# A mixture-of-experts decoder layer on one core: slot weights in the experts' middle layer, the last pair's rows by a one-hot product, the branch at the end, shorter planned waits

## The chip, the cores and the metric

One core of a Trainium2 chip. The time is the device time of one execution in microseconds (us); where several runs are shown, their median. The engines are TensorE (PE, with its weight loads as PEld), VectorE (DVE), ScalarE (ACT), GpSimd (POOL) and SyncE (SP), which here issues the DMA transfers. Each engine works through its own list of instructions in order, and semaphores tie the lists together.

## The reference, cut to what matters

One layer of a decoder over 512 tokens of 1024 channels. An input projection feeds three token mixers (RWKV-7, block-sparse attention, an S5 state space), their outputs are gated, summed and projected; a layer norm follows. Then a router picks one of four groups and in it two of eight experts for each token:

```
def rwkv7_mixer(...): y = wkv7_scan(r, decay, k, v, -kk, kk * a); group norm over heads; (y + bonus) * g
merged = gates0 * (y_a @ w_up_rwkv) + gates1 * (y_b @ w_up_moba) + gates2 * (y_c @ w_up_ssm)
x = layer_norm(alpha * x + merged @ w_out)
weight = p_group * softmax(top2(e_logits))                # two per token
hid = silu(xb @ w_gate[e]) * (xb @ w_up[e])               # expert: 1024 -> 256
y[token] += (hid @ w_down[e]) * weight                    # both experts of a token
x = layer_norm(alpha * x + y)
```

The weight is a number per token and expert, so it may be multiplied into the hidden row as well as into the output row. All is float32; large products are split in a high and a low part of a shorter format and done as three products.

## The kernel before, in words

**The mixers.** The projections with the three mixers take the first 612 us. TensorE's list is written out in a fixed order by a small planner (`Trunk.run`): several generators, such as `rwkv`, `rwkv_ends` and `rwkv_next`, put out their work and yield a planned wait in us. The planner's clock is `PE.t`, which each matmul advances by columns x passes / 2400. When no generator is due, it takes the next piece of *fill*: gate and up-projection matmuls that nothing waits for, three per 128x128 block of split weights (`xhi,whi`, `xlo,whi`, `xhi,wlo`; later with `y`, then `b`, operands). When the fill is used up, the clock is set ahead and TensorE waits. The fill's weights are split into `whi` on ScalarE and `wlo` on GpSimd (line 304 and 305), a few ahead.

RWKV runs in two halves of four heads. In each, `rwkv_inv` inverts 32x32 blocks on DVE (31 steps of a product, L601, and a sum, L602, then transposes into TT and DF, L605 and L607), yields `46.0`, and has TensorE use DF; `rwkv_chain` carries the state S through eight chunks and writes Ys; `rwkv_post` normalises Ys by group, yields 21.0, transposes it on TensorE and adds into yfA (L717 to L719, over a buffer `yt`). `merge_parts` reads the results yd of the other two mixers back through a buffer `yf`, eight times, and splits each into hi (ACT) and lo (POOL: ylo, blo).

```
for s in range(31):  ... v.tensor_tensor(tm, LA[...], TL[...], op=mult); v.tensor_tensor(TL[...], TL[...], tm, op=add)
v.transpose(DF[:32], TT[:32, :, :32])
yield 46.0
```

**The experts.** After the output projection, norm and routing (612 to 696 us), 32 experts run as 16 pairs; each expert has 64 places, and a pair fills the 128 partitions. `slots()` makes tables by one-hot matmuls: for each place the slot row (`dst`, two rows per token) and the token (`src`). GpSimd gathers a pair's tokens two pairs ahead (`fetch`), TensorE turns them (`turn`), `hidden` runs the first matmuls and the middle layer, `outputs` the second, and an indirect DMA scatters the 128 rows to `ybuf` in DRAM. Weights (`expert_weights`: up 2 x 2 MB, down 2 x 1 MB per pair) stream through slots on SP's queue, in 1 MB transfers. An expert with more than 64 tokens is finished in `more_blocks`, behind a branch on a number `nov` read from SBUF; with these inputs it is 0. `combine` then reads the two rows of each token back, adds them to x1 by matmuls with two diagonal matrices of the weights (`dg`), and normalises.

## Time and profile before

| | |
|---|---|
| median of 3 runs | 978.24 us (973.08 to 980.92) |
| the profiled execution | 970.03 us, span 968.3 us |
| mean granted TensorE clock | 0.971 of full speed |
| TensorE busy | 862.3 us (89%) |
| DVE, ACT, POOL busy | 547.6, 320.6, 306.4 us |
| expert weights | 96 transfers of 1 MB |

Times in the rows are from the start of the span. A timeline row has start, duration, engine, line, operation and names, and in brackets the engine's idle time before it with what ended it. The time is about 2 us longer than the span, which is what lies around it.

### The profile page before, as it was taken

Reading aid. Unit: us, or ns where it says so; the run is one execution under the profiler, and the core shown is the slowest. Engines: PE = TensorE matmul, PEld = TensorE weight load, DVE = VectorE, ACT = ScalarE, POOL = GpSimd, SP = SyncE. Lnnn points to the kernel's source line nnn. Section 1 sums busy time; section 2 is a strip of 40 time slices with the busy share of each in tenths; the row PEclk is TensorE's granted clock in tenths of the full one; section 3 lists DMA queues with packets and bytes.
Section 4 is the critical chain, followed back from the end, with each engine's and each line's share of the span. In section 5 each row is a group of like instructions: output and inputs, shape, how many; then the busy total and the mean of one; then the engine's idle time right before and its main releaser. Section 6 shows DMA issues by size and latency. Waiting matters only on the chain. (4 is left out here: it accounts for less than half of the span.)

```text
span 968.3 us, 13711 instructions
## 1 busy us (share of the span) xinstructions
PE 862.3 (89%) x4988; PEld 577.7 (60%) x4988; DVE 547.6 (57%) x1348; ACT 320.6 (33%) x626; POOL 306.4 (32%) x265
## 2 busy tenths in 40 slices
PE   6998897899999999799999968988979997879775
PEld 4876665677877776678788756866643333323232
DVE  6999998345325899625996776548631110101117
ACT  4244545576337157321532202232001110101012
POOL 6462512232453333622355213553001111101003
PEclk9999999999999999999999988999999999989998
DMA  6821322141442212321256312589798999999955
GB/s 209 166 97 55 66 86 57 50 141 59 138 131 66 87 66 71 125 78 56 89 154 207 120 65 66 175 340 386 290 367 346 413 417 420 419 419 418 409 200 187
DMA packets 71016, 186.62 MB, mean 193 GB/s; under 512 B 22027, under 2 KB 22027, under 8 KB 58624
## 3 DMA queue, kind: packets, MB, share of 16 engines
q1 hardware_dynamic: 66048, 175.77, 50.5%
q0 software_dynamic: 4896, 9.93, 2.7%
q8 instruction: 41, 0.67, 0.3%
q14 instruction: 31, 0.25, 0.1%
HBM read 171.29 MB, written 22.28 MB: 200 GB/s over the span
## 5 line engine op out<-in xcount | busy, mean ns | idle before, releaser
L305 POOL TENSOR_TENSOR wlo<-raw,whi 128x512 fp32r<-128x512 f32 x156 | 214.8, 1382 | 345.1 <-ACT whi L304 334.2
L175 PE MATMUL bank<-xhi,whi 128*128 128x512 f32 x400 | 168.9, 422 | 8.6 <-ACT whi L304 7.5
L175 PE MATMUL bank<-xhi,wlo 128*128 128x512 f32 x400 | 159.9, 400 | 7.6 <-POOL wlo L305 7.3
L304 ACT ACTIVATE whi<-raw 128x512 fp32r<-128x512 f32 x156 | 97.5, 628 | 200.4 <-PE bank L175 136.1
L175 PE MATMUL bank<-xlo,whi 128*128 128x512 f32 x400 | 159.7, 399 | 2.0 <-DVE xlo L305 1.9
L175 PE MATMUL bank<-we,xgT 128*64 128x512 f32 x512 | 127.5, 624 | 17.5 <-DMA we<-in_ex 17.5
L175 PEld LDWEIGHTS bank<-we,xgT 128*64 128x64 f32 x512 | 42.0, 144 | 98.7 <-issue 72.2
L175 PEld LDWEIGHTS bank<-xhi,whi 128*128 128x128 f32 x400 | 77.5, 194 | 28.9 <-ACT whi L304 7.9
L175 PEld LDWEIGHTS bank<-xhi,wlo 128*128 128x128 f32 x400 | 76.8, 192 | 27.8 <-POOL wlo L305 11.4
L175 PEld LDWEIGHTS bank<-xlo,whi 128*128 128x128 f32 x400 | 77.0, 193 | 17.9 <-DVE xlo L305 4.4
L1618 DVE SCALAR_TENSOR_TENSOR eth<-eth,bank 128x256 f32<-128x256 f32 x16 | 6.7, 421 | 129.1 <-ACT eth L1617 129.0
L175 PE MATMUL bank<-we,hT 128*64 128x512 f32 x256 | 59.2, 598 | 8.4 <-ACT hT L1629 7.3
L1617 ACT ACTIVATE eth<-bank 128x256 f32<-128x256 f32 x16 | 6.1, 384 | 162.4 <-PE bank L175 162.4
L1593 POOL DMA_INDIRECT xg<-x1d,src x14 | 14.2, 1018 | 121.3 <-PE bank L179 98.9
L1642 POOL DMA_INDIRECT ybuf<-we,dst x16 | 16.2, 1009 | 94.5 <-issue 42.1
L175 PEld LDWEIGHTS bank<-we,hT 128*64 128x64 f32 x256 | 18.9, 136 | 38.4 <-issue 25.0
L1641 DVE COPY we<-bank 128x512 f32<-128x512 f32 x16 | 11.1, 691 | 54.1 <-PE bank L175 54.1
L175 PE MATMUL bank<-wlo,mxhi 128*128 128x512 f32 x64 | 25.6, 400 | 3.2 <-POOL wlo L305 3.2
L784 ACT ACTIVATE s<-s,st 128x128 f32<-128x128 f32 (+3 forms) x32 | 17.8, 557 | 31.2 <-DVE st L783 31.2
L175 PE MATMUL bank<-whi,mxhi 128*128 128x512 f32 x64 | 25.9, 405 | 0.9 <-ACT whi L304 0.9
L175 PE MATMUL bank<-yhi,whi 128*128 128x512 f32 x64 | 25.8, 404 | 0.3 <-ACT yhi L304 0.3
L175 PE MATMUL bank<-ylo,whi 128*128 128x512 f32 x64 | 25.3, 395 | 0.8 <-POOL ylo L305 0.8
(466 smaller groups left out, 1596.8 us busy)
## 6 DMA issues: line engine op xcount, KB each, us to landing
we<-in_ex SPq DMA_DIRECT2D x96, 1024.0 KB, 21.7
raw<-in_wt SPq DMA_DIRECT2D x100, 256.0 KB, 2.7
sg<-th SPq DMA_DIRECT2D x24, 256.0 KB, 3.3
raw<-in_up SPq DMA_DIRECT2D x24, 256.0 KB, 2.8
th<-sg SPq DMA_DIRECT2D x24, 256.0 KB, 2.9
raw<-in_wout SPq DMA_DIRECT2D x16, 256.0 KB, 2.8
we<-ybuf SPq DMA_DIRECT2D x8, 512.0 KB, 8.9
xraw<-in_xT SPq DMA_DIRECT2D x8, 256.0 KB, 5.6
```

Source lines behind the costliest of these rows:

```text
L175: return self.eng.matmul(out, lhsT=lhsT, rhs=rhs, **kw)
L304: nc.scalar.activation(hi, src, AF.Copy)
L305: (eng or nc.gpsimd).tensor_tensor(lo, src, h, op=OP.subtract)
L784: self.nc.scalar.activation(s[:, :n], s[:, :n], AF.Exp, bias=st[:, 0:1], accum_out=st[:, 1:2])
L1593: self.nc.gpsimd.indirect_dma_start(out=self.xg, out_offset=None, in_=self.x1d, in_offset=bass.IndirectOffsetOnAxis(ap=self.src[:, col:col ...
L1617: nc.scalar.activation(th, ph[:, :256], AF.Tanh, scale=0.5)
L1618: v.scalar_tensor_tensor(th, th, 1.0, ph[:, :256], op0=OP.add, op1=OP.mult)
L1641: v.tensor_copy(y[:, 512:], py)
L1642: d = nc.gpsimd.indirect_dma_start(out=self.ybuf, out_offset=bass.IndirectOffsetOnAxis(ap=self.dst[:, col:col + 1], axis=0), in_=y, in_off ...
```

## The change

Five things are changed. Planned wait: 46 becomes 29 in the first half and 25 in the second; and the buffer yf alternates between its own tag and that of yt. Slot weights: a second one-hot table (`pw`, `wsl`) gives each place its weight, which takes the place of the factor 0.5 in the middle layer; so the combination is a plain sum. Slot rows: ybuf is filled with zeros early on, by one memset and eight writes. The last pair's rows are not scattered: a one-hot matrix `hot` (place x token) multiplies them onto x1 in PSUM, and DVE adds the slot rows of the other pairs to x1; the order of the last weights is changed with it. The branch for larger experts now stands behind the last output and, if taken, does the end again. Beside these, products with a [128, 1] operand are written as tensor_scalar with scalar operands in place of scalar_tensor_tensor.

```diff
@@ -248,10 +248,10 @@
                 table = self.slots()
-                self.experts(xT, table)
+                late = self.experts(xT, table)
                 rt.close()
-            self.more_blocks()
-            self.combine()
+            self.fp = e(self.pool("fin", "right"))
+            self.more_blocks(*self.combine(*late))
@@ -377,8 +377,8 @@
         for c in (3.0, 12.0, 768.0) if n == 1 else ():
-            nc.vector.scalar_tensor_tensor(t, y, y, xe, op0=OP.mult, op1=OP.mult)
-            nc.vector.scalar_tensor_tensor(y, t, -c, y, op0=OP.add, op1=OP.mult)
+            nc.vector.tensor_scalar(t, y, y, xe, op0=OP.mult, op1=OP.mult)
+            nc.vector.tensor_scalar(y, t, -c, y, op0=OP.add, op1=OP.mult)
@@ -605,7 +605,7 @@
         v.transpose(DF[:32], TT[:32, :, :32])
-        yield 46.0
+        yield (29.0, 25.0)[hf]
@@ -812,6 +812,7 @@
         ap = self.ap
+        self.ybuf = self.scr.tile([2 * T, D], F32, name="ybuf")
@@ -837,6 +838,11 @@
+
+        z = ap.tile([P, D], F32, name="zero")
+        self.nc.gpsimd.memset(z, 0.0)
+        for i in range(2 * NT):
+            self.nc.sync.dma_start(self.ybuf[i * P:(i + 1) * P], z)
@@ -1222,7 +1228,7 @@
             for j in range(4):
-                yf = self.rp.tile([P, T], F32, name="yf", tag="zxwa")
+                yf = self.rp.tile([P, T], F32, name="yf", tag=("zxwa", "yt")[j % 2])
@@ -1259,8 +1265,8 @@
             nc.scalar.activation(y, t, AF.Sqrt, scale=-0.5)
-            v.scalar_tensor_tensor(t, y, y, xe, op0=OP.mult, op1=OP.mult)
-            v.scalar_tensor_tensor(y, t, 1.5, y, op0=OP.add, op1=OP.mult)
+            v.tensor_scalar(t, y, y, xe, op0=OP.mult, op1=OP.mult)
+            v.tensor_scalar(y, t, 1.5, y, op0=OP.add, op1=OP.mult)
@@ -1316,7 +1322,7 @@
                 nm = lp.tile([P, 1], F32, name="lnm", tag="lnm", bufs=2)
-                v.scalar_tensor_tensor(nm, mean, -1.0, rs, op0=OP.mult, op1=OP.mult)
+                v.tensor_scalar(nm, mean, -1.0, rs, op0=OP.mult, op1=OP.mult)
@@ -1488,6 +1496,22 @@
+        ge, gs = new("ge", NT, 4), new("gs", NT)
...
+        v.tensor_tensor(w12[:, :, 0], gs, dd, op=OP.mult)
+        v.tensor_tensor(w12[:, :, 1], w12[:, :, 0], p2, op=OP.mult)
@@ -1523,39 +1547,26 @@
         v.tensor_copy(self.ov, ov)
-        hc = new("hc", NT, 2, NCOL)
+        hc, hw = new("hc", NT, 2, NCOL), new("hw", NT, 2, NCOL)
...
             v.tensor_tensor(hc[:, tt], cf[:, 0, tt].unsqueeze(2).to_broadcast([P, 2, NCOL]), io[:, None, :NCOL].to_broadcast([P, 2, NCOL]), op=OP.is_equal)
+            v.tensor_tensor(hw[:, tt], hc[:, tt], w12[:, tt].unsqueeze(2).to_broadcast([P, 2, NCOL]), op=OP.mult)
...
         def table():
-            pt = self.bank()
-            for r in range(2):
-                for i in range(8):
-                    self.pe.matmul(pt[64 * r:64 * r + 64, :NCOL // 2], lhsT=hr[:, i // 2, i % 2], rhs=hc[:, i // 2, i % 2, r::2], start=(i == 0), stop=(i == 7))
+            pt, pw = self.bank(), self.bank()
+            for h, ps in ((hw, pw), (hc, pt)):
+                for r in range(2):
+                    for i in range(8):
+                        self.pe.matmul(ps[64 * r:64 * r + 64, :NCOL // 2], lhsT=hr[:, i // 2, i % 2], rhs=h[:, i // 2, i % 2, r::2], start=(i == 0), stop=(i == 7))
+            v.tensor_scalar(self.wsl, pw[:, :NCOL // 2], 0.5 / ALPHA, None, op0=OP.mult)
...
-        ge, gs = new("ge", NT, 4), new("gs", NT)
...
-        v.tensor_tensor(w12[:, :, 0], gs, dd, op=OP.mult)
-        v.tensor_tensor(w12[:, :, 1], w12[:, :, 0], p2, op=OP.mult)
@@ -1606,20 +1617,24 @@
         return xT
...
-    def hidden(self, xT, w):
-        nc, v, ep = self.nc, self.nc.vector, self.ep
+    def first(self, xT, w):
...
                 self.pe.matmul(ph[pp], lhsT=xT[:, k, pp], rhs=w[r][:, k * 512:(k + 1) * 512], start=(k == 0), stop=(k == KD - 1))
-        th = ep.tile([P, 256], F32, name="eth", tag="eth", bufs=2)
+        return ph
+
+    def hidden(self, ph, col, th=None):
+
+        nc, v, ep = self.nc, self.nc.vector, self.ep
+        th = th or ep.tile([P, 256], F32, name="eth", tag="eth", bufs=2)
...
         v.scalar_tensor_tensor(th, th, 1.0, ph[:, :256], op0=OP.add, op1=OP.mult)
-        v.scalar_tensor_tensor(th, th, 0.5, ph[:, 256:], op0=OP.mult, op1=OP.mult)
+        v.scalar_tensor_tensor(th, th, self.wsl[:, col:col + 1], ph[:, 256:], op0=OP.mult, op1=OP.mult)
         return th
...
-    def outputs(self, col, th, w):
+    def second(self, th, w, between=None):
@@ -1627,6 +1642,8 @@
         nc.scalar.activation(hT, pt, AF.Copy)
+        if between:
+            between()
@@ -1639,6 +1656,12 @@
                 v.tensor_copy(y[:, 512:], py)
+        return y
+
+    def outputs(self, col, th, w):
+
+        nc = self.nc
+        y = self.second(th, w)
@@ -1667,79 +1690,102 @@
-        self.ybuf, self.scattered = self.scr.tile([2 * T, D], F32, name="ybuf"), []
+        self.scattered = []
         late, more = None, []
-        for p in range(NP + 1):
-            if p < NP:
-                w = self.expert_weights(p, 0)
-            if late:
+        for p in range(NP):
+            if p == NP - 1:
+                down = self.expert_weights(p - 1, 1)
+            w = self.expert_weights(p, 0)
+            if 0 < p < NP - 1:
...
                 more = self.expert_weights(1, 1, (0,))
-            if p < NP:
-                th = self.hidden(xT.pop(0), w)
+            if p == NP - 1:
+                last = self.expert_weights(p, 1)
+                self.outputs(p - 1, late, down)
+            ph = self.first(xT.pop(0), w)
...
                 self.fetch(2)
+            th = self.hidden(ph, p, self.slot(4, 0, (256,)) if p == NP - 1 else None)
...
                     self.fetch(p + 2)
-            if p:
...
-
-    def more_blocks(self):
+        return late, last
+
+    def more_blocks(self, lnv, hot, y):
...
         nov = nc.values_load(self.ov[0:1, 0:1], min_val=0, max_val=NOV)
...
-                for r in range(2):
...
-
-    def combine(self):
-
+        with tc.If(nov > 0):
...
+                    for r in range(2):
...
+            for tt in range(NT):
+                nc.sync.dma_start(self.x1[tt], self.x1d[tt * P:(tt + 1) * P])
+            self.finish(lnv, hot, y)
+
+    def combine(self, th, down):
...
+
+        nc, v, g, pe, fp = self.nc, self.nc.vector, self.nc.gpsimd, self.pe, self.fp
+        lnv = self.ln_vectors(self.we1, 1, tag="we3_1")
+        ti, hot, sf = fp.tile([P, T], I32, name="ti"), fp.tile([P, T], F32, name="hot"), fp.tile([P, 1], F32, name="srcf")
+        g.iota(ti, pattern=[[1, T]], base=0, channel_multiplier=0)
+        g.tensor_copy(hot, ti)
+        v.tensor_copy(sf, self.src[:, NP - 1:NP])
+        v.tensor_scalar(hot, hot, sf, None, op0=OP.is_equal)
+        y = self.finish(lnv, hot, lambda: self.second(th, down))
+        return lnv, hot, y
+
+    def finish(self, lnv, hot, y):
         nc, v, g, pe = self.nc, self.nc.vector, self.nc.gpsimd, self.pe
-        lnv = self.ln_vectors(self.we1, 1, tag="we3_1")
-        dg = self.slot(2, 1, (NT, 2, P))
-        for tt in range(NT):
-            for i in range(2):
-                v.tensor_scalar(dg[:, tt, i], self.ident, self.w12[:, tt, i:i + 1], 1.0 / ALPHA, op0=OP.mult, op1=OP.mult)
...
         halves = [slice(512 * c, 512 * c + 512) for c in range(2)]
-        r = []
+        yt = []
         for tt in range(NT):
-            r.append([self.bank() for _ in range(2)])
+            yt.append(self.slot((5, 6, 0, 1)[tt], 0, (2, D)))
+            nc.sync.dma_start(yt[tt], yv[tt * P:(tt + 1) * P])
+            for i in range(2):
+                v.tensor_tensor(self.x1[tt], self.x1[tt], yt[tt][:, i], op=OP.add)
+        r = [[] for _ in range(NT)]
+
+        def rows(tt):
             for c, cs in enumerate(halves):
+                r[tt].append(self.bank())
...
+
+        y = y() if callable(y) else y
         for tt in range(NT):
-            yt = self.slot((4, 5, 6, 0)[tt], 0, (2, D))
+            rows(tt)
...
             for c, cs in enumerate(halves):
-                nc.sync.dma_start(yt[:, :, cs], yv[tt * P:(tt + 1) * P, :, cs])
-                for i in range(2):
-                    pe.matmul(r[tt][c], lhsT=dg[:, tt, i], rhs=yt[:, i, cs], start=False, stop=(i == 1))
+                pe.matmul(r[tt][c], lhsT=hot[:, tt * P:(tt + 1) * P], rhs=y[:, cs], start=False, stop=True)
...
                 nm = self.ep.tile([P, 1], F32, name="nm", tag="nm", bufs=2)
-                v.scalar_tensor_tensor(nm, mean, -1.0, rs, op0=OP.mult, op1=OP.mult)
+                v.tensor_scalar(nm, mean, -1.0, rs, op0=OP.mult, op1=OP.mult)
             for c, cs in enumerate(halves):
-                o = yt[:, 0, cs]
+                o = yt[tt][:, 0, cs]
```

Below is TensorE's order around the second half's inverse, before (the transposes of the first half's Ys, then fill, then the matmuls on DF):

```order
L179 MATMUL bank<-ident,Ys 128x128 x4
L175 MATMUL bank<-z_xg,g_2904 128x512
...
L175 MATMUL bank<-bhi,whi 128x512
L175 MATMUL bank<-blo,whi 128x512
L175 MATMUL bank<-bhi,wlo 128x512
L175 MATMUL bank<-DF,AM 32x32 x16
```

and now:

```order
L179 MATMUL bank<-ident,Ys 128x128 x4
L175 MATMUL bank<-z_xg,g_2915 128x512
...
L175 MATMUL bank<-xhi,whi 128x512
L175 MATMUL bank<-xlo,whi 128x512
L175 MATMUL bank<-xhi,wlo 128x512
L175 MATMUL bank<-DF,AM 32x32 x16
```

Between the two stood 201 fill matmuls (93 x, 96 y, 12 b), and now 102 (x). Ahead of the first half's matmuls on DF there are 75 fewer than before, ahead of the second half's 162 fewer. At the end of the second half's chain TensorE had no fill before:

```order
L175 MATMUL Y<-S_5744,Q 64x64 x4
L179 MATMUL bank<-ident,Ys 128x128 x4
L175 MATMUL bank<-z_xg,g_2904 128x512
```

and now, with 102 fill matmuls (54 y, 48 b) between the chain's last product and Ys:

```order
L175 MATMUL bank<-bhi,whi 128x512
L175 MATMUL bank<-blo,whi 128x512
L175 MATMUL bank<-bhi,wlo 128x512
L179 MATMUL bank<-ident,Ys 128x128 x4
L175 MATMUL bank<-z_xg,g_2915 128x512
```

DVE's order in the second inverse, at the first L717 of the first half, before (in brackets the engines and DMA queues that it waits for):

```order
L601 TENSOR_TENSOR TM<-LA,F_4829 64x220 [waits DVE_49]
L602 TENSOR_TENSOR F_4829<-F_4829,TM 64x10x22 [waits DVE_49]
L717 TENSOR_SCALAR yt<-bank,vec 128x512 [waits PE_49]
```

and now:

```order
L601 TENSOR_TENSOR TM<-LA,F_4737 64x240 [waits DVE_49]
L717 TENSOR_SCALAR yt<-bank,vec 128x512 [waits DMAHW1_49,DMAHW4_49,DMAHW0_49,DMAHW5_49,PE_49,Pool_49]
L602 TENSOR_TENSOR F_4737<-F_4737,TM 64x12x20 [waits DVE_49]
```

The instruction stands two steps later in the inverse, and waits for GpSimd and four DMA queues, those of yf's earlier contents. GpSimd's list now, around those splits:

```order
L305 TENSOR_TENSOR ylo<-yf,yhi 128x512 [waits PE_49] x2
L305 TENSOR_TENSOR wlo<-raw,whi 128x512 [waits DMAHW3_49,PE_49,Activation_49]
L305 TENSOR_TENSOR blo<-yf,bhi 128x512 [waits DMAHW7_49,Activation_49]
L305 TENSOR_TENSOR blo<-yf,bhi 128x512 [waits DMAHW0_49,Activation_49]
L305 TENSOR_TENSOR wlo<-raw,whi 128x512 [waits DMAHW4_49,PE_49,Activation_49]
L305 TENSOR_TENSOR blo<-yf,bhi 128x512 [waits DMAHW3_49,Activation_49]
L305 TENSOR_TENSOR blo<-yf,bhi 128x512 [waits DMAHW4_49,Activation_49]
```

The two ylo and the four blo now stand together with two weight splits among them.

## Rows read from the trace of the kernel before

**Rows 1.** The page, part 1: busy us (share of the span) xinstructions.

```profile
PE   862.3 (89%) x4988; PEld 577.7 (60%) x4988; DVE 547.6 (57%) x1348; ACT 320.6 (33%) x626; POOL 306.4 (32%) x265
```

**Rows 2.** Stretches: length, busy of each engine, PEclk, DMA share, GB/s.

```profile
735.00:932.00 197.00, 171.54 (x772) 63.01 (x768) 29.80 (x61) 27.60 (x55) 25.30 (x25) 0.97 0.99 405
```

**Rows 3.** The same view, a stretch of 5 us in the experts' start.

```profile
730.00:735.00 5.00, 4.53 (x28) 2.00 (x26) 1.44 (x3) 1.36 (x3) 1.02 (x1) 1.00 0.46 141
```

**Rows 4.** TensorE's waits, 540 to 600 us: total us, times, longest.

```profile
PE bank L179 <- DVE Ys L366: 8.9, 1, 8.9
PE bank L175 <- DVE S L688: 2.0, 2, 1.2
PE bank L175 <- POOL ylo L305: 0.8, 1, 0.8
```

**Rows 5.** Stretches again, behind the chain's end.

```profile
585.00:590.00 5.00, 5.00 (x16) 3.18 (x15) 4.49 (x6) 0.63 (x1) 1.27 (x1) 0.69 0.00 0
```

**Rows 6.** Timeline of DVE: the last step of the second inverse.

```profile
505.57 1.23 DVE L607 STREAM_TRANSPOSE DF<-TT 32x1024 f32<-32x1024 f32 x1
```

**Rows 7.** Timeline of TensorE: fill ahead of the second half's matmuls on DF.

```profile
504.70 0.39 PE L175 MATMUL bank<-yhi,whi 128*128 128x512 f32 x1
...
529.76 0.62 PE L175 MATMUL bank<-DF,AM 32*32 32x32 f32 x14
```

**Rows 8.** Timeline of DVE: the first L717, within the second inverse.

```profile
481.25 0.81 DVE L717 TENSOR_SCALAR yt<-bank,vec 128x512 f32<-128x512 f32 x1
```

**Rows 9.** Timeline of GpSimd: one ylo, the first and last of four blo.

```profile
473.29 1.29 POOL L305 TENSOR_TENSOR ylo<-yf,yhi 128x512 fp32r<-128x512 f32 x1 [4.14 <-PE bank L179]
...
482.85 1.30 POOL L305 TENSOR_TENSOR blo<-yf,bhi 128x512 fp32r<-128x512 f32 x1 [2.25 <-ACT bhi L304]
...
496.96 1.31 POOL L305 TENSOR_TENSOR blo<-yf,bhi 128x512 fp32r<-128x512 f32 x1 [2.38 <-ACT bhi L304]
```

**Rows 10.** Timelines of SP's queue and of ScalarE: a load of yf, its split.

```profile
474.61 0.33 SPq L1226 DMA_DIRECT2D yf<-ydC  x1
...
477.35 0.63 ACT L304 ACTIVATE yhi<-yf 128x512 fp32r<-128x512 f32 x1 [1.31 <-DMA yf<-ydC]
```

**Rows 11.** Timelines of SP's queue and of TensorE: last loads, first use of U.

```profile
41.78 1.47 SPq L1036 DMA_DIRECT2D U<-ud  x3
...
66.72 2.08 PE L175 MATMUL bank<-U,CtT 128*64 128x64 f32 x64
```

**Rows 12.** Timeline of TensorE: the table's matmuls.

```profile
705.45 2.87 PE L175 MATMUL bank<-hc,hr 128*64 128x24 f32 x29 [2.25 <-DVE hc L1530]
```

**Rows 13.** Single lines: ns min/median/max, first and last start us, forms.

```profile
L1262 DVE SCALAR_TENSOR_TENSOR rsy<-rsx,rst x4: 205/556/1096, 948.0 to 962.0; 128x1 f32<-128x1 f32 x4
...
L1263 DVE SCALAR_TENSOR_TENSOR rsx<-rsy,rsx x4: 158/426/1183, 948.2 to 962.5; 128x1 f32<-128x1 f32 x4
...
L1321 DVE TENSOR_TENSOR x<-x,lnv x3: 1225/1226/1226, 651.0 to 670.4; 128x1024 f32<-128x1024 f32 x3
```

**Rows 14.** The page, part 5: busy us, mean ns, idle before and releaser.

```profile
L1617 ACT ACTIVATE eth<-bank 128x256 f32<-128x256 f32 x16 | 6.1, 384 | 162.4 <-PE bank L175 162.4
```

**Rows 15.** Timelines of TensorE, then DVE: the last pair and the end.

```profile
914.80 7.08 PE L175 MATMUL bank<-we,xgT 128*64 128x512 f32 x30 [0.82 <-DMA we<-in_ex]
...
926.47 0.44 PE L179 MATMUL bank<-ident,eth 128*128 128x128 f32 x2
...
932.97 1.52 PE L175 MATMUL bank<-x,ident 128*128 128x512 f32 x3 [1.42 <-DVEq L1696]
...
931.59 0.69 DVE L1641 COPY we<-bank 128x512 f32<-128x512 f32 x1 [4.32 <-PE bank L175]
...
943.42 0.70 DVE L1735 BATCH_NORM_STATS2 lst<-bank 128x6 f32<-128x512 f32 x1 [11.14 <-PE bank L175]
...
963.74 1.41 DVE L1752 SCALAR_TENSOR_TENSOR we<-we,rsx,lnv 128x512 f32<-128x512 f32 x2
```

**Rows 16.** SP's own queue waits, 900 us to the end.

```profile
SPq L1696 <- SPq L1696: 5.6, 2, 5.1
```

More of the change, by code (lines that the diff above doesn't have):

```diff
@@ L1352, in out_proj @@
         self.ranks(tt - 1)
-        sel = self.rt.tile([P, 1, 4, CAP], F32, name="sel1")
+        sel = self.rt.tile([P, 1, 4, CAP], F32, name="sel1", tag="sel1")
         self.select(sel, 0, tt - 1)
@@ L1402, in route_consts @@
         self.w12 = keep("w12", NT, 2)
+        self.wsl = keep("wsl", NCOL // 2)
         self.dst = keep("dst", NCOL // 2, dt=I32)
@@ L1581, in first_gather @@
         self.nc.gpsimd.memset(self.xg, 0.0)
-        sel = self.rt.tile([P, 1, 4, CAP], F32, name="sel2")
+        sel = self.rt.tile([P, 1, 4, CAP], F32, name="sel2", tag="sel1")
         xT = [self.ep.tile([P, KD, P], F32, name="xgT", tag="xgT", bufs=2) for _ in range(2)]
@@ L1713, in combine @@
-    def combine(self):
-        nc, v, g, pe = self.nc, self.nc.vector, self.nc.gpsimd, self.pe
-        lnv = self.ln_vectors(self.we1, 1, tag="we3_1")
-        dg = self.slot(2, 1, (NT, 2, P))
-        for tt in range(NT):
-            for i in range(2):
-                v.tensor_scalar(dg[:, tt, i], self.ident, self.w12[:, tt, i:i + 1], 1.0 / ALPHA, op0=OP.mult, op1=OP.mult)
+        with tc.If(nov > 0):
+            with ExitStack() as ctx:
+                for m in range(NOV // 2):
+                    if m:
+                        ctx.enter_context(tc.If(nov > 2 * m))
+                    w = []
+                    for r in range(2):
+                        i = 1 + 2 * m + r
+                        e = nc.values_load(self.ov[0:1, i:i + 1], engines=[mybir.EngineType.SP], min_val=0, max_val=NE - 1)
+                        row = self.a["ex"][bass.ds(e, 1)].rearrange("o p f -> (o p) f")
+                        w.append([self.slot(2 + r, 0), self.slot(4 + r, 1)])
+                        nc.sync.dma_start(w[r][0], row[:, :KD * 512])
+                        nc.sync.dma_start(w[r][1], row[:, KD * 512:])
+                    up, down = zip(*w)
+                    col = NP + m
+                    self.fetch(col)
+                    xT = self.turn()
+                    self.outputs(col, self.hidden(self.first(xT, up), col), down)
+            for tt in range(NT):
+                nc.sync.dma_start(self.x1[tt], self.x1d[tt * P:(tt + 1) * P])
+            self.finish(lnv, hot, y)
```

42 lines of the change are left out of this document (14 added, 28 removed).

## The prediction

> **What bounds the kernel now.** The page's first part [rows 1] shows TensorE busy 89% of the span, so I looked first for the time in which it is not. Of the stages, only the experts' has another limit: between 735 and 932 us the DMA engines are 99% busy at 405 GB/s [rows 2], and there TensorE waits for weights. Everywhere before 735, time is won by closing TensorE's gaps, and everything that comes earlier there comes earlier at the end as well, because that stream of weights is started by slots that TensorE frees: in 730:735 the DMA engines are 46% busy [rows 3]. The third view, TensorE's waits around the end of the RWKV chain [rows 4], shows the largest closed hole: 8.9 us until DVE has normalised Ys, 2.0 us in the last steps of the chain, 0.8 us behind it. The granted clock that follows is low [rows 5]: 0.69 of full speed in 585:590, thus between the two levels. There is no fill work left there. But there was plenty before: DVE ends the second inverse (the transpose into DF) at 506.80 [rows 6], and TensorE's first matmul on DF stands at 529.76 [rows 7], 23 us later, all that time with fill. The planner gave the inverse 46 us of fill by its own count; fill really takes 0.232 us each (108 of them from 504.70 to the DF matmul at 529.76, [rows 7]), against 0.213 us in the planner (512 columns at 2400 per us).
>
> **1. Shorter planned waits.** The order shows 75 fewer fills ahead of the first DF matmul and 162 fewer ahead of the second; 102 of the fills now stand between the chain's end and the transposes of Ys. 102 x 0.232 = 23.7 us of work lie where 8.9 us of idle time were, so that hole closes, as do the 2.0 and 0.8. With the slow clock after it (6.8 us from 583.2 to 590 at about 0.64 lose 2.4) that is 8.9 + 2.0 + 0.8 + 2.4 = **14.1 us** off.
>
> What is late next: the second DF matmul comes 162 x 0.232 = 37.6 us earlier, at 492.2. DVE's second inverse starts behind the first chain, which has 63 fills fewer ahead of it, so it comes 14.6 us earlier and ends at 506.8 - 14.6 = 492.2. The cover is gone to the last tenth: whatever holds DVE up in this inverse now holds TensorE.
>
> And something does. The change gives every second yf buffer the tag of yt, and the first L717 of the first half writes yt, in the middle of DVE's second inverse. In the order that instruction now waits for GpSimd: for the last of the four blo splits. Before, L717 ran at 481.25 [rows 8], but the blo splits ran from 482.85 to 498.27, one per 4.7 us [rows 9], as each load of yf waited for the split ahead (2.7 us from the load's issue to the next ACT split, [rows 10]). With two buffers they go in pairs. On the clock of before: ylo at 473.29 and 474.6 [rows 9], loads of B0 and B1 at 474.7 and 475.9, their blo splits to 480.6, loads of B2 and B3 behind these, a weight split between, the last blo ends near 486.8. DVE reaches L717 two inverse steps later than before, some 1.5 us, at 482.7: it stands for **4.1 us**, and TensorE with it. The clock after a gap cost 2.4 above, where the gap was over twice as long; I take 1.5. Bounds: 0 when the splits are through in time, 15.6 when they keep the old pace (498.3 - 482.7). I take 4.1 + 1.5 = +5.6, since two buffers make the pairs but nothing makes them early. Queued behind L717 on DVE is the whole rest of the inverse, and behind that TensorE's DF matmuls.
>
> **2. Zeros for the slot rows.** A memset on GpSimd and eight 512 KB writes on SP's queue, four of them ahead of and among the loads of U. 4 MB at 405 GB/s are 10.4 us. The last U load is issued by 43.25 and TensorE first reads U at 66.72 [rows 11]; that and the weights already split are the cover. If it were gone, up to 10 us would show. I take +0.7 (0 to 4), mostly for the memset beside a busy DVE.
>
> **3. The table.** Sixteen more matmuls of the kind hc,hr, 29 of whose 32 records took 2.87 us, so 3.2 in all, behind a wait of 2.25 us for DVE [rows 12]; and four more products on DVE ahead of them. The weights of the slots were computed early before too (the order shows them ahead of the table in both), so that move costs nothing: DVE's other work around it hides it. Unpaced the new matmuls cost 1.6, at the measured pace 3.2; with the products 0.7 more. What stands behind them is the gather for pair 2, in a stretch where the DMA engines run dry later [rows 3], so it passes to the end. +2.5 (0 to 3.9).
>
> **4. One-column products.** L1262 takes 0.21 us at best and 1.10 at worst, L1263 0.16 and 1.18 [rows 13], eight in the tail, about 4.6 us in all; at their minima 1.45. As tensor_scalar (one tensor input) I expect the minima: -3.2 in the tail, and -0.3 for the like ones in the out projection.
>
> **5. The last pair and the tail.** Down weights of pair 14 now go ahead of pair 15's: two transfers of 1 MB, 2 x 2.6 = 5.2 us at 405 GB/s. Pair 15's first matmuls, which started at 914.80 when their weights landed [rows 15], start at 920.0 and end at 927.1 (7.08 us). The middle layer is no longer hidden by pair 14's output: a tanh of 0.38 us [rows 14] and two products, with the hops some 1.7. From the transposes to the copied y took 926.47 to 932.28 [rows 15], 5.8 us. So y is there at 934.6, 2.3 us later. From there the scatter, its landing and the loads of its rows are gone; DVE has eight adds instead (1.23 us each by L1321's row, [rows 13], 9.8), then what it did from the first BN_STATS at 943.42 to 965.15 [rows 15], 21.7 - 3.2 = 18.5. 934.6 + 9.8 + 18.5 = 962.9, against 965.15: -2.2. The diagonal matrices and their 16 matmuls go, the eight one-hot matmuls lie beside DVE.
>
> The branch moves behind the last output. Before it cost TensorE 1.42 us of idle time at 932.97 [rows 15]; at the end it lies beside the landing of the last output on all engines but SP, which waits for that landing anyway. SP stood there 5.1 us before [rows 16], beside weights still landing. +1 (0 to 4, those 5.1 less about 1 for the landing). [...]
>
> **Sum.** -14.1 + 5.6 + 0.7 + 2.5 - 0.3 - 2.2 + 1.0 = -6.8. Against the profiled execution's 970.03 (span 968.3) that is 963.2. The median of the runs shown is 978.24, 8.2 above the profiled one; on that scale the forecast is 971.4, **971**.
>
> **Rivals.**
> - *The block does not happen*: GpSimd is through with blo when DVE comes to yt. For it: DVE gets there only after a group norm that also moves. Against: the loads hang on each other. -6.8 - 5.6 = -12.4, 965.8 on the runs' scale.
> - *The change does not do what it says*: the hole closes but its time is lost elsewhere, as another DVE wait inside the chain or in the stream of weights, if the transfers, not the slots, set its end. For it: 99% busy [rows 2]; against it: the dry stretch ahead [rows 3]. The 8.5 go, +1.7, 979.9.
> - *Slower*: DVE stands at yt until the fill behind is used up. The weight split ahead of the last two blo splits needs a buffer that TensorE frees; if it is not free, each weight costs TensorE 12 fills, 2.8 us, before it comes. With eight of them DVE stands 22 us, TensorE idles as long, and the clock costs 3: -14.1 + 22 + 3 + 1.7 = +12.6, 990.8. It decides from about 12 us on (no gain) and 19 (slower by 1%). Against it: that split is three weights ahead of TensorE's place and there are six buffers.
>
> **Numbers.** Forecast 0.50, no block 0.25, gain lost 0.15, slower 0.10. One per cent of 978, the least that these runs can tell from none, is 9.8 us. The second case lies beyond it nearly whole (0.23), and of the first the part in which the block or the table cost 3 us less (0.12): faster 0.35. Slower takes the last case and a little of the third: 0.12. The rest, 0.53, is within 1%. The range reaches from the second case with a run below the median (965.8 - 7) to the third with its bounds (979.9 + 3): 959 to 983. The forecast's own range is 966 to 977.
>
> **What would show it.** Right: no wait for Ys at the chain's end; one new wait of TensorE for the DF transpose of about 4 us, with DVE idle as long before L717 on GpSimd; the merge's end about 8.5 us earlier; and the tail's first BN_STATS near 942 with eight DVE adds about it. L1262 and L1263 near their minima. Wrong: TensorE waiting for U, DVE idle beyond 8 us at L717, or a stretch without any engine after the last output lands.

## The result: 972.9 us, and the profile after

The changed kernel takes 972.86 us (median of 20 runs), the kernel before 978.73 (20 runs beside them): a ratio of 0.992, 95% interval 0.989 to 0.995, so 0.8% off. One of the 20 runs of the changed kernel was a slow one (1219.86 us, clock 0.651) and is left out of the ratio and of all that follows. The forecast was 971. The profiled execution took 973.63 us, span 971.9, clock 0.953, and is thus *longer* than the profiled one of before (970.03). Much of the change can be read in it all the same; the difference has one main cause, which lies nowhere in the forecast.

The page's first part (columns as in [rows 1]), then TensorE's waits at 490 to 520 and 540 to 600 us (those of [rows 4]; total us, times, longest):

```profile
PE 873.6 (90%) x5004; PEld 588.6 (61%) x5004; DVE 559.9 (58%) x1355; ACT 321.9 (33%) x626; POOL 311.7 (32%) x267
```

```profile
PE bank L175 <- DVE DF L607: 2.8, 1, 2.8
...
PE bank L175 <- DVE th L1244: 0.5, 1, 0.5
```

The wait of 8.9 us for Ys is gone, with the 2.0 and 0.8 beside it. One wait is new, for the DF transpose. What made DF late is in the timelines of GpSimd and of DVE (start, length, then the idle time ahead and what ended it):

```profile
463.70 2.55 POOL L305 TENSOR_TENSOR ylo<-yf,yhi 128x512 fp32r<-128x512 f32 x2 [3.34 <-PE bank L179]
468.51 2.64 POOL L305 TENSOR_TENSOR blo<-yf,bhi 128x512 fp32r<-128x512 f32 x2 [0.17 <-ACT bhi L304]
473.41 1.28 POOL L305 TENSOR_TENSOR wlo<-raw,whi 128x512 fp32r<-128x512 f32 x1 [2.26 <-ACT whi L304]
474.65 2.54 POOL L305 TENSOR_TENSOR blo<-yf,bhi 128x512 fp32r<-128x512 f32 x2
```

```profile
472.49 0.41 DVE L601 TENSOR_TENSOR TM<-LA,F 64x240 f32<-64x240 f32 x1
477.22 0.81 DVE L717 TENSOR_SCALAR yt<-bank,vec 128x512 f32<-128x512 f32 x1 [4.33 <-DMA raw<-in_wt]
```

DVE stops in the middle of the inverse for 4.33 us. The profile names a transfer, but L717 does not read `raw`; it starts at 477.22, and the last blo ends at 477.19. That is the read of yf in the buffer that L717 wants to write. The pairs are there too: four blo, and a weight split between, in 8.7 us, where they took 15.4 before [rows 9].

Now the stretches (columns as in [rows 2]; the sixth number after the length is the granted clock), first behind the new wait, then at 330 us:

```profile
500.00:505.00 5.00, 3.37 (x37) 2.92 (x38) 2.46 (x3) 0.59 (x1) 0.00 (x0) 0.72 0.20 52
505.00:510.00 5.00, 5.00 (x40) 3.90 (x39) 0.00 (x0) 1.90 (x3) 1.27 (x1) 0.50 0.26 47
510.00:515.00 5.00, 5.00 (x44) 3.89 (x44) 0.68 (x1) 0.63 (x1) 1.28 (x1) 0.76 0.17 61
...
330.00:340.00 10.00, 9.86 (x41) 7.62 (x41) 5.20 (x8) 0.00 (x0) 1.80 (x2) 0.58 0.27 92
340.00:350.00 10.00, 10.00 (x45) 8.41 (x44) 4.80 (x6) 0.63 (x1) 0.89 (x1) 0.50 0.00 1
350.00:360.00 10.00, 10.00 (x54) 8.21 (x52) 7.86 (x21) 7.25 (x15) 1.67 (x2) 0.90 0.08 28
```

The clock falls to 0.50, the lower of the two levels in these traces (1.00 and 0.50), behind the new wait, and again for some 20 us at 330 us. In the trace of before all of 330 to 360 us is granted 1.00; one of its rows:

```profile
340.00:350.00 10.00, 9.01 (x55) 7.34 (x54) 8.89 (x20) 6.93 (x15) 2.34 (x2) 1.00 0.08 29
```

TensorE is *busy* there; it only runs slower, so no list of waits shows this stretch. The same place in TensorE's timeline, after and then before:

```profile
329.05 1.13 PE L175 MATMUL bank<-E,bones 128*128 128x512 f32 x2 [1.31 <-DVE E L520]
330.11 3.27 PE L175 MATMUL bank<-AR,BK 64*128 64x128 f32 x16
...
334.88 3.09 PE L175 MATMUL bank<-AR,BK 64*128 64x128 f32 x16
```

```profile
327.85 1.13 PE L175 MATMUL bank<-E,bones 128*128 128x512 f32 x2 [1.31 <-DVE E L520]
328.90 2.44 PE L175 MATMUL bank<-AR,BK 64*128 64x128 f32 x16
...
332.17 1.71 PE L175 MATMUL bank<-AR,BK 64*128 64x128 f32 x16
```

The same order of work and the same idle 1.31 us; before, the two groups take 2.44 and 1.71 us at a granted 1.00, after, 3.27 and 3.09, at 0.50 from 332 us on. At a matmul behind this dip (on z_xwa, 364.03 before, 373.21 after) the profiled runs are 9.2 us apart; 1.2 of them are there ahead of it (327.85, 329.05), so the dip costs 8.0. With both taken out the profiles are near the forecast: the first matmul behind the merge stands at 612.12 before and 611.77 after, 9.5 us earlier net of 1.2 and 8.0.

The end, by timelines of TensorE, DVE and SP's queue, and SP's own waits from 900 us on (answers to [rows 15, 16]):

```profile
920.70 8.78 PE L175 MATMUL bank<-we,xgT 128*64 128x512 f32 x30 [3.27 <-DMA we<-in_ex]
...
931.95 5.35 PE L175 MATMUL bank<-we,hT 128*64 128x512 f32 x16 [0.53 <-ACT hT L1644]
...
937.35 0.69 DVE L1658 COPY we<-bank 128x512 f32<-128x512 f32 x1 [6.49 <-PE bank L175]
937.96 7.27 DVE L1767 TENSOR_TENSOR x<-x,we 128x1024 f32<-128x1024 f32 x6
945.14 1.29 DVE L1781 BATCH_NORM_STATS2 lst<-bank 128x6 f32<-128x512 f32 x2
...
962.42 2.87 DVE L1798 SCALAR_TENSOR_TENSOR we<-we,rsx,lnv 128x512 f32<-128x512 f32 x2
965.19 0.88 SPq L1799 DMA_DIRECT2D out<-we  x2
```

```profile
SPq L1723 <- SPq L1723: 3.3, 1, 3.3
```

y is there at 938.04. The matmuls ahead of it ran at a low clock in this execution, 0.83 at 920 to 930 us:

```profile
920.00:930.00 10.00, 8.78 (x30) 2.61 (x30) 0.07 (x1) 0.38 (x1) 0.00 (x0) 0.83 0.87 339
```

From the last output's issue (966.07) to the span's end pass 5.8 us, where 2.8 passed before (965.51 to 968.3): SP's 3.3 us at the branch, L1723, lie in the open.

### The profile page after: what moved, and what is told of

Read it like the earlier page. It is cut to its first block, busy times and chain, and to the rows that moved or that the text cites. A ratio compares the mean times of both kernels' runs of the same rounds, so it can differ in the third digit from the quotient of the medians.

```text
span 971.9 us, 13743 instructions
## 1 busy us (share of the span) xinstructions
PE 873.6 (90%) x5004; PEld 588.6 (61%) x5004; DVE 559.9 (58%) x1355; ACT 321.9 (33%) x626; POOL 311.7 (32%) x267
## 4 chain that ended last, share of the span: by engine, by line
PE 46%; DVE 26%; DMA 19%; issue 4%; ACT 2%; POOL 1%; SPq 0%; POOLq 0%; DVEq 0%; ACTq 0%
PE bank L175 43%; DMA we<-in_ex 15%; PE bank L179 2%; DVE TT L605 1%; POOL wlo L305 1%; DMA ybuf<-we,dst 1%; DVE Zt L1009 1%; DVE sc L1112 1%; DVE Z L1008 1%; DMA xg<-x1d,src 1%; PE Y L175 1%; DVE x L1767 1%; DVE F L602 1%; DVE Z L1010 1%; DVE TM L601 1%
## 5 line engine op out<-in xcount | busy, mean ns | idle before, releaser
L305 POOL TENSOR_TENSOR wlo<-raw,whi 128x512 fp32r<-128x512 f32 x156 | 218.2, 1403 | 356.9 <-ACT whi L304 337.8
L175 PE MATMUL bank<-xhi,whi 128*128 128x512 f32 x400 | 174.1, 435 | 9.7 <-ACT whi L304 7.0
L175 PE MATMUL bank<-xhi,wlo 128*128 128x512 f32 x400 | 163.5, 409 | 1.4 <-POOL wlo L305 1.1
L175 PE MATMUL bank<-xlo,whi 128*128 128x512 f32 x400 | 163.2, 408 | 0.3 <-DVE xlo L305 0.3
L175 PEld LDWEIGHTS bank<-xhi,whi 128*128 128x128 f32 x400 | 79.5, 199 | 31.4 <-ACT whi L304 7.5
L175 PEld LDWEIGHTS bank<-xhi,wlo 128*128 128x128 f32 x400 | 79.0, 197 | 21.4 <-POOL wlo L305 4.0
L175 PEld LDWEIGHTS bank<-xlo,whi 128*128 128x128 f32 x400 | 79.6, 199 | 15.6 <-DVE xlo L305 1.7
L1658 DVE COPY we<-bank 128x512 f32<-128x512 f32 x16 | 11.1, 691 | 59.4 <-PE bank L175 59.4
L781 DVE SCALAR_TENSOR_TENSOR s<-dist,bank 128x128 f32<-128x128 f32 (+3 forms) x32 | 15.4, 481 | 18.0 <-PE bank L175 17.9
```

What stands on the lines that cost most here:

```text
L175: return self.eng.matmul(out, lhsT=lhsT, rhs=rhs, **kw)
L305: (eng or nc.gpsimd).tensor_tensor(lo, src, h, op=OP.subtract)
L781: v.scalar_tensor_tensor(s[:, :n], self.dist[:, o:o + n], -2.0 ** -(2 * j + par + 1), ps[:, :n], op0=OP.mult, op1=OP.add)
L1658: v.tensor_copy(y[:, 512:], py)
```

## The experiments

**Two groups of runs.** The runs of before (23 beside the first experiments) and of each kernel that keeps the order at 330 us fall in two groups, with medians some 6 to 11 us apart and few runs between. The split is less clear in the 20 runs of before beside the changed kernel: four of them (977.76 to 979.21) lie between. Of the profiled executions, those with the clock at 0.50 at 335 to 345 us belong to the longer group, those with 1.00 to the shorter. Of the other runs only the mean granted clock is on record: in the changed kernel 0.958 to 0.967 for the shorter ones, 0.948 to 0.955 for the longer, but for one of 0.959. It does not part every run (waits_only's of 970.86 us has 0.963), so runs without a profile are put to a group by their time alone. Medians and numbers of runs:

| kernel | shorter | longer |
|---|---|---|
| before, 23 runs | 975.0 (14) | 983.3 (9) |
| before, the 20 beside the changed kernel | 975.5 (11) | 981.8 (9) |
| changed | 964.7 (7) | 974.4 (12) |
| waits_only | 960.3 (4) | 970.6 (2) |
| waits_yt | 965.0 (5) | 970.7 (1) |
| after_one_yf | 962.9 (4) | 971.3 (8) |
| after_no_branch | 963.0 (4) | 974.2 (8) |
| after_scatter | 964.6 (5) | 973.8 (6) |
| after_no_hw | 962.8 (5) | 968.7 (1) |

Like with like, the change is worth 10.3 us (shorter) or 8.9 (longer) against the 23 runs, 10.8 or 7.4 against the 20. The medians of all runs show 5.9, because that of the changed kernel lies in its longer group (12 of 19) and that of before at the top of its shorter one (11 of 20). Parts of the change are therefore compared within the shorter group. The experiments were run in four sets, each beside runs of before; the shorter group of these has medians from 973.9 to 975.0, so a difference under about 1 us between sets says nothing.

The profiles give a second measure, which the dip at 330 us does not touch: the time from the matmul on z_xwa behind it to the first matmul behind the merge. It is 248.1 us before and 233.4 in waits_only, from these rows:

```profile
374.88 3.02 PE L175 MATMUL bank<-z_xwa,wa 64*128 64x512 f32 x8
...
608.31 0.39 PE L175 MATMUL bank<-whi,mxhi 128*128 128x512 f32 x1
```

In waits_yt it is 238.1, in after_one_yf 234.7, in the changed kernel 238.6.

**waits_only**: the kernel before, with the planned wait alone.

```diff
-        yield 46.0
+        yield (29.0, 25.0)[hf]
```

> The kernel before with one edit: the planned wait of the inverse is 29 and 25 in place of 46 (yf keeps its one buffer). Theory A (the fill that was kept back closes the hole at the chain's end, and the shared yt buffer takes part of it back): 11 to 14 us faster than before, ratio 0.986 to 0.989, no wait of TensorE for Ys, and L717 not stopped on GpSimd. Rival B (the gain of the whole change comes from its end: no last scatter, DVE adds): ratio 1.000 within 0.003.

Measured 961.03 us (957.78 to 970.86, 6 runs), ratio 0.984 (0.979 to 0.990); 14.7 less than before in the shorter group, and 14.7 by the second measure. TensorE has no wait at 540 to 600 us, and DVE none for GpSimd at L717. The shorter wait alone beats the whole change, by 4.4 us in the shorter group and 3.8 in the longer.

**waits_yt**: that, and the second tag of yf.

```diff
-                yf = self.rp.tile([P, T], F32, name="yf", tag="zxwa")
+                yf = self.rp.tile([P, T], F32, name="yf", tag=("zxwa", "yt")[j % 2])
```

> As waits_only, and yf alternates between its own tag and that of yt, as in the change. Theory A: 4 to 6 us slower than waits_only (DVE stands some 4 us at L717, TensorE behind it at the DF matmuls), so 7 to 9 us faster than before, ratio 0.991 to 0.993. Rival C (the second yf buffer gains as much on SP's queue as the wait at L717 costs): the same as waits_only within 2 us.

Measured 965.04 (964.22 to 970.74, 6), ratio 0.988 (0.984 to 0.993): 4.7 more than waits_only in the shorter group, and 4.7 by the second measure. TensorE waits for DF again, so rival C is out and the shared buffer is what costs:

```profile
PE bank L175 <- DVE DF L607: 3.3, 1, 3.3
```

**after_one_yf**: the whole change with the one tag of before.

```diff
-                yf = self.rp.tile([P, T], F32, name="yf", tag=("zxwa", "yt")[j % 2])
+                yf = self.rp.tile([P, T], F32, name="yf", tag="zxwa")
```

> The changed kernel with yf in its one old buffer (the yt tag undone). Theory A: 3 to 6 us faster than the changed kernel (972.9), ratio to before 0.986 to 0.989; DVE does not stop at L717. Rival C: the same as the changed kernel, 0.992, as the loads of yf then block SP's queue for as long.

Measured 970.49 (959.44 to 975.39, 12), ratio 0.988 (0.983 to 0.992): 1.8 less than the changed kernel in the shorter group (4 runs), 3.1 in the longer. That is less than the 3 to 6 expected, and than the 4.7 from the other side. Part of what the stop costs is given back later: in the profiles the changed kernel needs 3.9 us more by the second measure, but 1.3 less from there to the end of the span (360.1 against 361.4), a stretch in which the weights set the pace for the most part (DMA share 1.02 at 735 to 900 us in both).

**after_no_branch**: the changed kernel without the blocks for experts over 64 tokens (left out).

```diff
-            self.more_blocks(*self.combine(*late))
+            self.combine(*late)
```

> The changed kernel without the branch for larger experts (left out: the work for experts with more than 64 tokens, of which these inputs have none). In the changed kernel 5.8 us pass from the last output's issue (966.1) to the end of the span (971.9), before it were 2.8. Theory A (the branch at the very end is in the open): 3 us faster than the changed kernel, ratio to before 0.989, 2.8 us from the last issue to the end. Rival D (the branch lies beside the landing of the last output): within 1 us of the changed kernel.

Measured 973.21 (962.3 to 975.86, 12), ratio 0.993 (0.989 to 0.997). The profile shows 3.4 us from the last issue to the end in place of 5.8, but the groups hide it: 1.7 less in the shorter, 0.2 less in the longer. By its runs alone this decides nothing; after_early_branch, below, agrees with the profile.

**waits_warm** and **after_warm**: the dip, by moving fill on waits_only and on after_one_yf. Some 24 fill matmuls go ahead of the second half's `bones` and between its AR,BK groups.

```diff
-        yield (3.0, 10.0)[hf]
+        yield (6.0, 10.0)[hf]
...
-            yield 0.6
+            yield (1.3, 0.6)[hf]
```

> waits_only (the kernel before with the shorter planned waits) with 24 fill matmuls of the first half moved ahead: the planned wait before the second pair of bones matmuls is 6 in place of 3, so that TensorE does not stand idle there (1.3 us), and between the groups of AR,BK matmuls that follow there are 6 fills in place of 3. The runs of every kernel so far fall into two groups some 9 us apart (before: 972 to 978 and 983 to 986), and four of six profiles show the granted clock at 0.50 from 331 to 352 us, behind that idle stretch, and two do not. Theory E (the two groups are this fall of the clock, and the idle stretch with the small matmuls behind it brings it): the upper group is gone, all runs at 958 to 963, clock 1.00 from 330 to 350. Rival F (the fall comes of itself, whatever TensorE does there): two groups as before, 960 and 970.

> The same move of 24 fills in the changed kernel with one yf buffer (after_one_yf), which had four runs at 959 to 963 and eight at 969 to 975. Theory E: all runs at 959 to 964, ratio to before 0.983 to 0.985. Rival F: two groups as before, median near 970.

Measured 959.57 (959.14 to 962.17, 6), ratio 0.981 (0.977 to 0.985), and 964.24 (961.28 to 967.48, 6), ratio 0.986 (0.981 to 0.990). All twelve runs are shorter than the longer group (968.7 and up for after_one_yf), eleven of them clearly, and the clock at 325 to 355 us is 1.00 in both profiles. Rival F is out.

The pair, run side by side, shows one thing more. after_warm has all of the change but the second buffer, and takes 4.7 us *more* than waits_warm. In their profiles, which are 2.4 us apart, 353.0 and 355.4 us pass from the first matmul behind the merge (600.73; 599.62) to the last output's issue (953.68; 955.0), and from there to the end 6.5 and 2.8. By these profiles the rest of the change gains 2.4 us there, and 3.7 are lost behind the last output, where the branch now stands.

**after_scatter**: after_one_yf with the end of before: the last pair scattered, the old weight order, the branch ahead of the combination. Slot weights, zeros and the eight adds stay.

```diff
-            self.more_blocks(*self.combine(*late))
+            self.more_blocks()
+            self.combine()
...
-                pe.matmul(r[tt][c], lhsT=hot[:, tt * P:(tt + 1) * P], rhs=y[:, cs], start=False, stop=True)
```

> after_one_yf with the last pair scattered as all others, its weights in the old order, and the branch ahead of the combination as before; slot weights, zeros and the eight adds on DVE stay. From the forecast's step 5: y 2.3 us earlier, but then scatter, landing (4 us) and loads (4 us) before the first adds, which no longer lie ahead: DVE's adds then start near 941 and the end is at 941 + 9.8 + 18.5 = 969, 5 to 6 us later than after_one_yf in the same group of runs. Rival G (the one-hot end gains nothing, since TensorE's clock is low there and the branch stands in the open): within 2 us of after_one_yf.

Measured 970.35 (963.23 to 975.09, 11), ratio 0.991 (0.987 to 0.995): 1.7 more than after_one_yf in the shorter group, of another set. So the new end, with its branch, gains only about that over this one, and rival G is nearer than the 5 to 6. DVE's timeline of this kernel shows what the scatter costs:

```profile
931.21 5.05 DVE L1751 TENSOR_TENSOR x<-x,we 128x1024 f32<-128x1024 f32 x4 [9.91 <-DMA we<-ybuf]
```

y was copied at 921.30; DVE idles 9.91 us until its rows have come back. This is not quite the end of before: there TensorE adds the rows, and the first BN_STATS follows 11.1 us behind y's copy (932.28, 943.42); here DVE's adds come first, and it follows after 14.9 (936.17).

**after_no_hw**: after_one_yf without the weight table; a constant stands for the slot weights, and 16 matmuls and four products are left out.

```diff
-            v.tensor_scalar(self.wsl, pw[:, :NCOL // 2], 0.5 / ALPHA, None, op0=OP.mult)
+            v.memset(self.wsl, 0.5 / ALPHA)
```

> after_one_yf without the second one-hot table: the slots' weights are a constant, so the 16 matmuls hw,hr and DVE's four products are left out, and the outputs are weighted wrongly. Forecast's step 3: 2.5 us faster than after_one_yf in the same group of runs, the gather for pair 2 lands 3 us earlier. Rival H (the stream of weights sets the end anyway): the same within 1 us.

Measured 962.9 (961.62 to 968.73, 6), ratio 0.985 (0.981 to 0.989); 962.8 against 962.9 in the shorter group. The table costs nothing at the end that these runs can tell, as rival H has it. In its profile the gather for pair 2 is issued 99.1 us behind the merge's end (698.07, 599.0), in after_one_yf's 101.4 (710.39, 608.99); at the last output's issue the two are 354.5 and 354.9 us behind it. So 2.3 us are won, and all but 0.5 lost again. The changed kernel's stretch:

```profile
735.00:900.00 165.00, 144.42 (x660) 52.18 (x658) 24.82 (x45) 22.17 (x45) 23.39 (x24) 0.97 1.02 418
```

The DMA engines move 418 GB/s with no time free (share 1.02), and 419 without the table.

**after_early_branch**: after_warm with the branch between the last pair's first matmuls and the combination.

```diff
+        self.more_blocks()
         y = self.finish(lnv, hot, lambda: self.second(th, down))
```

> after_warm with the branch for larger experts between the last pair's first matmuls and the combination, where TensorE waits for the middle layer anyway. after_warm needed 6.5 us from the last output's issue to the end of the span, waits_warm (branch ahead of the combination) 2.8. Theory A (3 to 4 us of the branch are in the open at the very end): 2.8 us from the last issue to the end and 2 to 4 us faster than after_warm (964.2), so 960 to 962. Rival D (it only changes places: SP and TensorE stop at it as long before the combination): within 1 us of after_warm.

Measured 962.13 (957.93 to 963.05, 6), ratio 0.985 (0.981 to 0.989): 2.1 less than after_warm, which was run in another set; from the merge's end to the end of the span its profile is 2.3 us shorter (357.2 against 359.5). From the last issue to the end pass 3.4 us (955.45 to 958.9) against 6.5 (953.68 to 960.2). TensorE waits 2.29 us there, 0.75 more than it waited anyway (1.54).

**after_gap** and **after_mix**: the two halves of the move apart, each on after_one_yf: the fill ahead of the `bones` products only, and the fill between the small groups only.

```diff
-        yield (3.0, 10.0)[hf]
+        yield (6.0, 10.0)[hf]
```

```diff
-            yield 0.6
+            yield (1.3, 0.6)[hf]
```

> after_one_yf with only the first of the two moves of fill: 6 in place of 3 planned before the second pair of bones matmuls, so that TensorE's 1.3 us of idle time there are filled; the groups of AR,BK matmuls keep 3 fills between them. Theory E1 (the idle stretch brings the fall of the clock): no run in the upper group, all at 960 to 966. Theory E2 (the small matmuls bring it): two groups as in after_one_yf (eight of twelve in the upper).

> after_one_yf with only the second move: 6 fills in place of 3 between the groups of AR,BK matmuls; the idle 1.3 us stay. Theory E1: two groups, most runs at 970. Theory E2: all runs at 960 to 966.

Measured 963.65 (958.93 to 965.07, 6), ratio 0.986 (0.982 to 0.990), all in the shorter group, as E1 has it; and 966.99 (965.7 to 972.84, 6), ratio 0.990 (0.987 to 0.994), which fits neither theory. TensorE's timeline of after_gap, and a stretch of each:

```profile
330.32 0.50 PE L175 MATMUL bank<-xhi,wlo 128*128 128x512 f32 x1 [1.16 <-POOL wlo L305]
...
332.73 1.88 PE L175 MATMUL bank<-E,bones 128*128 128x512 f32 x4
334.54 1.71 PE L175 MATMUL bank<-AR,BK 64*128 64x128 f32 x16
```

```profile
330.00:340.00 10.00, 9.68 (x55) 6.95 (x56) 7.14 (x10) 0.63 (x1) 4.93 (x4) 1.00 0.44 133
```

```profile
330.00:340.00 10.00, 8.87 (x35) 6.66 (x36) 5.76 (x8) 0.00 (x0) 3.75 (x3) 0.66 0.36 107
```

An idle of 1.16 us is still there in after_gap, but 2.4 us of full-width fill follow it, and the clock stays at 1.00. In after_mix the idle 1.3 us stands ahead of `bones` and AR,BK as before; the clock falls (0.66) but is back at 1.00 from 340 us on. So in these runs it was enough to fill the time ahead of `bones`, and in this profile more fill behind only shortens the fall. Six runs are few: of the 11 runs of before beside them only two are in the longer group. And after_gap also brings the four `bones` matmuls together. That the place of the idle time decides is thus the likeliest reading, but it is not shown by itself.

**waits_warm_ts**: waits_warm with the one-column products as tensor_scalar, the version that the runs pointed to (four such places).

```diff
-            v.scalar_tensor_tensor(t, y, y, xe, op0=OP.mult, op1=OP.mult)
+            v.tensor_scalar(t, y, y, xe, op0=OP.mult, op1=OP.mult)
```

> waits_warm with the change's tensor_scalar form for the products of [128, 1] operands (the two of rsqrt in the out projection, the two of the norm's second step, the two negated means). Forecast's step 4: L1262 and L1263 near 0.26 and 0.20 us each in the tail in place of up to 1.10 and 1.18, 2 to 3.5 us faster than waits_warm (959.6; ratio to before 0.9811), so ratio 0.977 to 0.979. Rival K (DVE's next two-input product then waits for GpSimd in their place): within 1 us of waits_warm.

Measured 958.26 (956.55 to 960.02, 6), ratio 0.979 (0.974 to 0.984), the shortest of all kernels here, 1.3 less than waits_warm. That lies between the 2 to 3.5 expected and the 1 of rival K, and as the two were run in different sets it is not clear of the noise. The single lines of L1262 (ns least, median, most; first and last start us), waits_warm and then this kernel:

```profile
L1262 DVE SCALAR_TENSOR_TENSOR rsy<-rsx,rst x4: 201/556/1094, 937.5 to 951.5; 128x1 f32<-128x1 f32 x4
```

```profile
L1262 DVE TENSOR_SCALAR rsy<-rsx,rst x4: 257/262/273, 935.9 to 948.6; 128x1 f32<-128x1 f32 x4
...
949.10 2.37 DVE L1752 SCALAR_TENSOR_TENSOR we<-we,rsx,lnv 128x512 f32<-128x512 f32 x2
```

In the trace of before the three long ones (0.61 at 951.59, 1.10 at 957.13, 0.50 at 961.98) start while GpSimd's products (L1748: 2.93 us from 950.47, 2.93 from 955.28, 2.87 from 960.82) run, the short one (0.20 at 947.99) does not. As tensor_scalar in the changed kernel (L1268) two of the four start beside such products (L1794: 6.20 us from 954.30, 3.26 from 961.48), at 958.08 and 961.87, and all four take 0.26 to 0.27. From the first BN_STATS to DVE's end pass 20.4 us, not 22.8. Of these 2.4 us 0.8 are no gain of the products: the wait for TensorE ahead of the second BN_STATS is 1.76 us in place of 2.60. Part goes into the last two products (L1752), 2.37 us in place of 1.42. In the changed kernel the same two (L1798) take 2.87 us from 962.42, beside GpSimd's last products (3.26 us from 961.48); in that of before [rows 15] they take 1.41, and GpSimd's have ended (963.69).

## Why the prediction came out

**1, the hole: right.** -14.1 forecast, -14.7 measured by waits_only, in its runs and by the second measure.

**1, the stop at L717: right in kind, the parts uneven.** DVE stood 4.33 us (4.1 forecast), TensorE 2.85 of them; the low clock behind it cost some 4 us by the stretches 500 to 515, and about 1.4 in waits_yt (0.92 at 490 to 500 and 0.91 at 500 to 510), where 1.5 were taken. Together +4.7 on the kernel before (+5.6 forecast), but only 1.8 to 3.1 in the whole change: the forecast let the whole of it pass to the end.

**2, the zeros: not told from none.** TensorE never waits for U. It reaches `bones` 1.2 us later than before in the profile, but waits_only, without zeros, reaches it 3.0 later. No run leaves out the zeros alone, so none shows the 0.7; the memset itself takes 0.94 us in the changed kernel (L843).

**3, the table: mis-sized.** +2.5 forecast, 0 measured. The step that failed is that the dry stretch at 730:735 [rows 3] passes what is late there to the end. The weights behind it make up about 2 us, as the rival on the stream of weights had it. Why these are made up, while the 14.7 us won ahead of the merge's end arrive in full, no run shows.

**4, the one-column products: right, smaller.** -3.2 forecast. In the changed kernel L1268 takes 0.26 us each time, 0.21 in L1269:

```profile
L1268 DVE TENSOR_SCALAR rsy<-rsx,rst x4: 256/260/267, 951.8 to 961.9; 128x1 f32<-128x1 f32 x4
...
L1269 DVE TENSOR_SCALAR rsx<-rsy,rsx x4: 190/204/215, 952.1 to 962.2; 128x1 f32<-128x1 f32 x4
```

waits_warm_ts shows 1.6 us on DVE, and 1.3 in the time, not clear of the noise. They do not reach the minima of [rows 13], and the last two products of all take 2.87 us, in place of 1.41 before.

**5, the last pair: y came 3.4 us late in the profile.** The start of the first matmuls was forecast to 0.7 us (920.0; 920.70), but after 3.27 us without weights they took 8.78 us, not 7.08, and the second 5.35, where the 16 of earlier pairs take 3.65. The forecast took the durations of the higher clock (7.08 us at 914.80, granted 1.00 at 915 to 920), though the trace of before had both: 8.48 us at 899.22 behind a wait of 3.54 (0.79 at 900 to 905). Nor is the lower one certain: in after_warm the same matmuls run at the forecast's pace behind as long a wait.

```profile
911.66 7.08 PE L175 MATMUL bank<-we,xgT 128*64 128x512 f32 x30 [3.24 <-DMA we<-in_ex]
...
921.22 3.65 PE L175 MATMUL bank<-we,hT 128*64 128x512 f32 x16 [0.53 <-ACT hT L1644]
```

There y is copied 13.95 us behind their start, where 14.6 were forecast. In the changed kernel's profile the first BN_STATS followed at 945.14, not near 942. What the new end gains over the scatter, with its branch, is 1.7.

**5, the branch: mis-sized.** +1.0 forecast, 2.1 by after_early_branch, 2.4 to 3.1 by the profiles' ends (5.8 and 6.5 us with it, 3.4 without it or with it earlier). The step that failed is that it lies beside the landing of the last output: SP's 3.3 us stand behind that output's issue, in the open. The forecast's 1 was too low. What the 3.3 us consist of, the trace does not show.

**The sum, like with like.** In the shorter groups the steps are -14.7 (waits_only against before), +2.6 (after_one_yf against waits_only: terms 2 to 5) and +1.8 (the second buffer), together -10.3. Forecast were -14.1, +1.7 and +5.6, together -6.8. The large terms are thus right in kind, and the stop is the one whose size is furthest off. The +2.6 is open: the warm pair has +4.7 for it, and the parts measured singly (table 0, one-column products -1.3, new end with branch -1.7) do not add up to it. The zeros and DVE's eight adds have no run of their own; the 14.9 us in place of 11.1 in after_scatter point to the adds.

**Not forecast: the dip at 330 us.** It takes about 4 of the 10 us back in the medians. That the median came within 2 us of the forecast is therefore in part luck: two misses cancel. The scale of the forecast hid the dip too, as the profiled execution of before had none and the runs shown, 8.2 us above it by their median, very likely did in part. That the clock falls is shown for the four profiled executions of the longer groups, and for a shorter time in after_mix; for the other runs it is inferred. That the moved fill keeps it up is shown by the five kernels with fill ahead of `bones` (1.00 at 325 to 355 us in their profiles): of their 30 runs at most one (967.48) may have had the dip, while 7 of 16, 2 of 11 and 5 of 11 runs of before beside them were in the longer group. Whether the changed kernel falls oftener than before (12 of 19, and 8 of 12, 8 of 12, 6 of 11 and 1 of 6 in its variants, against 9 of 20 and 9 of 23), and why it would, with the same idle time at the same place, stays open.

## What to carry to other kernels

A planned wait is best sized from measured durations, and cut until the producer's own end is the bound; then ask who else can stop that producer: with the shorter wait, the shared buffer cost 4.7 us here (waits_yt against waits_only). Where the clock falls, try full-width work between the idle time and the small matmuls (2.4 us of it in after_gap, whose clock stayed at 1.00), and price matmuls behind a wait at both clocks (7.08 and 8.78 us here). Ask what still covers a stall before it is moved to the very end (here SP's 3.3 us lay in the open). Where runs fall in two groups, compare within a group, or remove what splits them, before a few us are put down to an edit.

## What was not expected of the hardware

An idle of 1.31 us followed by two 128x512 matmuls and then AR,BK matmuls (64x128) was followed in the profile of the changed kernel by a clock of 0.50 for some 20 us, at a cost of 8.0 us, and in that of before by 1.00, with the same order of work there. An idle of 1.16 us followed by 2.4 us of fill was followed by 1.00 in the profile of after_gap. Matmuls behind a wait of 3.24 us for weights took 7.08 us in after_warm, the same ones behind 3.27 us 8.78 in the changed kernel. A scalar_tensor_tensor on one column (L1262, before) took 0.20 us away from GpSimd's products and 0.50 to 1.10 beside them, a tensor_scalar in its place (L1268, changed kernel) 0.26 to 0.27 either way.
